# Two of the four weight sums of a seven-product block: from VectorE to a plain load and an adding DMA

## The chip, the cores and the metric

The kernel runs on one core of one Trainium2 chip. A core has TensorE (PE in the profile; PEld is its weight load), VectorE (DVE), ScalarE (ACT), GpSimd (POOL) and SyncE (SP), which here only issues DMAs. The metric is device time in microseconds (us), the median of several runs of the same program.

## What is computed

One inference step of a two-layer transformer backbone on 640 tokens: 512 latent tokens (denoising) and 128 context tokens. Layer 0 mixes with latent-compressed attention and neighbourhood attention, layer 1 with grouped-query attention; each is followed by a gated feed-forward network, and a norm ends it all. The change touches the feed-forward networks:

```python
def swiglu(h, w_in, w_out):
    gate, up = jnp.split(h @ w_in, 2, axis=-1)
    return (jax.nn.silu(gate) * up) @ w_out

xp = xp + g2_p * swiglu(hp, w_ffn_in[l], w_ffn_out[l])
xs = xs + g2_s * swiglu(hs, w_ffn_in[l], w_ffn_out[l])
```

The model width is 1024 and the hidden width 2816, all in fp32.

## The kernel before

Activations stand with features on partitions, tokens on the free axis; the 640 tokens are taken as two halves of 320. fp32 products are made of three matmuls each: weight and activation are split into a rounded high part and the remainder, and high x high, high x low and low x high are added up in PSUM (`mm3`). A weight split is an ACT copy that rounds, and a DVE subtraction (`split`, L1367 and L1368).

**Blocks of seven products.** The first few hidden blocks of a layer are multiplied plainly (4 in layer 0, 3 in layer 1). From there on, a block's product with its 2 x 2 parts (two weight halves for two outputs, two token halves) is made of seven products instead of eight, after Strassen's scheme in the variant of Winograd. This needs sums of weight quarters. A block has a raw tile `ru` (up) and a raw tile `rg` (gate), each 128 x 1024 with two halves of m = 512 columns. `seven` makes four operands of them, each split into high and low: wX = `ru` itself; wW = right half of `rg`; wY = `s13`, two sums; wZ = `s24`, two further sums:

- L1176: s13 left = rg left + rg right
- L1177: s13 right = ru left + rg left
- L1180: s24 left = s13 right + rg right
- L1181: s24 right = s24 left + ru right

All four are DVE additions of 128 x m. `s13` and `s24` are tiles of one tag, `ws`, with two buffers. The matmuls of a block come in the order X, Y, (the W product of the block before, in `close`), Z, X, Z, Y; the profile calls their results `fg`, `fd`, `fu`.

`seven` is called for the blocks of the first feed-forward matrix (the loop from L1481 on: 18 blocks in layer 0, 19 in layer 1), and by `Block` in `ffn_out_seven` for the second matrix of layer 1: three passes (`PASSES`, over 3, 4 and 4 pairs of hidden blocks) with four blocks each, 12 blocks; there m is 384 in the first pass and 512 in the others, and the names in the profile end in o (`ruo`, `rgo`, `s13o`, `wYo`). In all there are 49 blocks.

**Transfers.** Raw weights are loaded by SP: `ru` into one of three buffers `raw`, `rg` into one of these or into a buffer `wr` (two in layer 0, one in layer 1). SP also writes the hidden activations of layer 1 to DRAM (`sp...`, L1398: seven operands a, D, N, b, c, C, E for each pair of blocks) and reads them back for the second matrix (`or...`, `again`, L1278; 320 KB each), a pass's set in turn as buffers come free. POOL issues a few stores of states and none in these stages. Products' operands wY, wZ, wX take turns in six buffers, so the splits run about one block ahead of their use.

**Order.** Each engine's queue is in order. The order in it is not that of the source: a planner sets it when the program is built, by its own times for each instruction and the order of the source as priority; in the trace, for instance, L1176 of block 4 stands on DVE ahead of L1174 of the same block. A load is put where its buffer comes free by the planner's times.

Of the kernel before, what the change touches and what calls it, by code (L numbers as in the profile page):

```python
# [11 lines left out]
F32 = mybir.dt.float32  # L12
F32R = mybir.dt.float32r
AF = mybir.ActivationFunctionType
ALU = mybir.AluOpType
# [3 lines left out]
P = 128  # L19
# [32 lines left out]
def body(ctx, tc, xT, vecs, crow, wm0, wm0g1, wm0g, wm1, wA, wNV, wNA, wMK, wMV, wOA, wGQ, wGK, wGV, wOC,  # L52
         wFI, wFO, wFO1, cckvT, ckrT, cnkT, cnv, cgkT, cgv, rpbp, tabM, tabK, tabG, maskN,
         yT, o_ckvT, o_krT, o_nkT, o_nv, o_gkT, o_gv):
    nc = tc.nc
    V, S, G = nc.vector, nc.scalar, nc.gpsimd
# [32 lines left out]
    def bank(name, kind="m"):  # L89
        if kind == "m":  # L90
            return psp.tile([P, 512], F32, tag="m", bufs=4, name=name)
        return ypool["pool"].tile([P, 512], F32, tag=kind, bufs=ypool["tags"][kind], name=name)
# [13 lines left out]
    def f(ap):  # L106
        return ap.bitcast(F32)
# [55 lines left out]
    def load(src, n, name):  # L163
        raw = rawp.tile([P, 1024], F32, tag="raw", name=name)
        nc.sync.dma_start(raw[:, :n], src)
        return raw[:, :n]
# [177 lines left out]
    def mod0(j, bk, load_):  # L344

        box = []

        def part(half):
            def run():
                if half == 0:  # L350
                    box.append(bk())
                psm, rs = box[0], load_(j, half)

                for g in range(4):
                    for b in range(2):
                        o = 512 * (g % 2) + 256 * b
                        rows = slice(64 * b + 32 * (g % 2), 64 * b + 32 * (g % 2) + 32)
                        PE.matmul(psm[rows, :256], scol[:, 4 * half + g, :], rs[g // 2][:, o:o + 256], start=half == 0 and g < 2,
                                  stop=half == 1 and g > 1, tile_position=(0, rows.start))
                if half == 1:  # L360
                    box.append(tp.tile([P, HT], F32, tag="u", bufs=7, name=f"modsb{j}"))
                    S.activation(box[1][:, :256], psm[:, :256], AF.Copy)
            return run

        def end():
            psm, sb = box
            for i in range(2):
                PE.matmul(psm[:, 4 * i:4 * i + 4], sb[:, i * P:(i + 1) * P], sel, start=True, stop=True)
            for i, t in enumerate(MOD0[j]):
                V.tensor_tensor(mods[0][:, t:t + 2, :], psm[:, 0:8].rearrange("p (a i b) -> p a i b", a=2, b=2)[:, :, i, :],  # L370
                                bc2(bmod(0, t, 2)), ALU.add)
        return [part(0), part(1), end]
# [139 lines left out]
    with tc.tile_pool(name="start", bufs=1) as big:  # L512
# [14 lines left out]
        m = [mod0(j, lambda j=j: bank(f"mod{j}", "m"), lambda j, half: [raws[j, half][:, q, :] for q in range(2)]) for j in range(4)]  # L527
# [91 lines left out]
    for kk in range(4):  # L619
# [3 lines left out]
        for j in range(2):  # L623
            k = 2 * kk + j
            a, b = wh[:, 512 * j:512 * (j + 1)], wl[:, 512 * j:512 * (j + 1)]
            for i in range(5):
                c0, c1 = P * i, P * i + P
# [256 lines left out]
    for h in range(8):  # L884
        p, r = divmod(h, 2)
# [116 lines left out]
    for h in range(8):  # L1002
        p, r = divmod(h, 2)
# [159 lines left out]
                w.append(unit(wFI[l, 0, i], 1024, f"wgu{l}_{i}", "vg"[i], pool=fp))  # L1163
        return ph, fk, dr, hd, fs, fp, w, (su, scratch), pre

    def seven(ru, rg, name, fp, split):

        n = ru.shape[-1]
        m = n // 2
        wX = split(ru, f"wX{name}")  # L1170
        t = fp.tile([P, 2, 512], F32R, tag="w4", bufs=2, name=f"wW{name}")
        wW = t[:, 0, :m], t[:, 1, :m]
        S.activation(wW[0], rg[:, m:], AF.Copy)
        V.tensor_tensor(wW[1], rg[:, m:], f(wW[0]), ALU.subtract)  # L1174
        s13 = fp.tile([P, 1024], F32, tag="ws", bufs=2, name=f"s13{name}")[:, :n]
        V.tensor_tensor(s13[:, :m], rg[:, :m], rg[:, m:], ALU.add)  # L1176
        V.tensor_tensor(s13[:, m:], ru[:, :m], rg[:, :m], ALU.add)  # L1177
        wY = split(s13, f"wY{name}")
        s24 = fp.tile([P, 1024], F32, tag="ws", bufs=2, name=f"s24{name}")[:, :n]
        V.tensor_tensor(s24[:, :m], s13[:, m:], rg[:, m:], ALU.add)  # L1180
        V.tensor_tensor(s24[:, m:], s24[:, :m], ru[:, m:], ALU.add)  # L1181
        wZ = split(s24, f"wZ{name}")
        return wX, wW, wY, wZ

    def ffn_out_seven(x, nxt, opened, ops, spilt, split, close, last):
# [6 lines left out]
        def raw(n, c0, m, name):  # L1192
            raws[0] += 1
            t = (rawp.tile([P, 1024], F32, tag="raw", name=name) if raws[0] % 4 else
                 fp.tile([P, 1024], F32, tag="wr", bufs=1, name=name))[:, :m]
            nc.sync.dma_start(t, wFO1[n, :, c0:c0 + m])
            return t
# [9 lines left out]
        def result(n, c, src, sign, end):  # L1207

            o = HALF[c][0]
            for c0, c1, i in HCOND[c]:  # L1210
                V.scalar_tensor_tensor(x[n][:, c0:c1], src[:, c0 - o:c1 - o],
                                       ng[:, n, i:i + 1] if sign < 0 else mods[1][:, G2 + n, i:i + 1], x[n][:, c0:c1], ALU.mult, ALU.add)
            if end:
                nrm.add(x[n], c)

        class Block:


            def __init__(self, i, n, c0):
                self.pairs, self.n, self.name = PASSES[i], n, f"o{i}_{n}"  # L1220
                self.end = i == len(PASSES) - 1
                self.m = m = P * len(self.pairs)
                ru, rg = raw(n, c0, 2 * m, f"ru{self.name}"), raw(n + 4, c0, 2 * m, f"rg{self.name}")
                self.wX, self.wW, self.wY, self.wZ = seven(ru, rg, self.name, fp, split)
                self.held = {}

            def go(self, ps, wt, j, what, first):
# [20 lines left out]
                    self.copy("p5", self.b5)  # L1248

            def p6(self):  # L1250
                self.go(self.g, self.wZ, 0, "N", False)
                self.copy("u2", self.g)

            def p2(self):
# [2 lines left out]
                result(self.n, 0, self.add("p1", b2), 1, self.end)  # L1257

            def p3(self):
                self.go(self.b5, self.wZ, 1, "c", False)  # L1260
                result(self.n, 1, self.add("u2", self.b5), 1, self.end)

            def p7(self, ready=True):
# [27 lines left out]
        prev, c0 = None, 0  # L1291
# [28 lines left out]
        e0, e1 = ends  # L1320
# [12 lines left out]
        for b in ends:  # L1333
# [4 lines left out]
                nrm.rstd(0)  # L1338
            t = weighed[b.n + 4] = tp.tile([P, HT], F32, tag="u", bufs=7, name=f"xw{b.n}")
            S.activation(t, x[b.n + 4][:, HT:T], AF.Copy, scale=vcol(V_NFIN + b.n + 4))  # L1340
        e0.go(e0.b5, e0.wZ, 1, "c", False)
        result(e0.n, 1, e0.b5, 1, True)
        e1.go(e1.b5, e1.wZ, 1, "c", False)
        sq = tp.tile([P, HT], F32, tag="u", bufs=7, name="fn1sqe")
        parts = []
        for c0, c1, i in HCOND[1]:
# [10 lines left out]
    def ffn(l, x, pend, hm, nxt, side, opened):  # L1357
# [3 lines left out]
        def split(src, name):  # L1361

            turn[0] += 1
            t = (wp, fp)[turn[0] % 2].tile([P, 2, 1024], F32R, tag="w", bufs=3, name=name)
            n = src.shape[-1]
            h, w_ = t[:, 0, :n], t[:, 1, :n]
            S.activation(h, src, AF.Copy)  # L1367
            V.tensor_tensor(w_, src, f(h), ALU.subtract)  # L1368
            return h, w_
# [5 lines left out]
        def product(ps, wt, w0, which, first):  # L1375
            for k, (h, l_) in enumerate(hm.operand(which)):
                a, b = [w[:, w0 + k * P:w0 + k * P + P] for w in wt]
                mm3(ps[:, :HT], a, b, h, l_, first and k == 0, k == 3, skip_group_check=not first)
# [102 lines left out]
        for fb in range(few, FB):  # L1481

            ru = load(wFI[l, fb, 1], 1024, f"wu{l}_{fb}r")
            if fb == few or l and fb % 2:
                rg = load(wFI[l, fb, 0], 1024, f"wg{l}_{fb}r")
            else:
                rg = fp.tile([P, 1024], F32, tag="wr", bufs=2 - l, name=f"wg{l}_{fb}r")
                nc.sync.dma_start(rg, wFI[l, fb, 0])
            wX, wW, wY, wZ = seven(ru, rg, f"{l}_{fb}", fp, split)

            g, b5, b2 = bank(f"fg{l}_{fb}"), bank(f"fd{l}_{fb}"), bank(f"fu{l}_{fb}", "y")
            up, sg = tmp(f"up{l}_{fb}"), tmp(f"sg{l}_{fb}")
            p1, p5, u1, g2 = [utile(f"{n}{l}_{fb}") for n in ("p1", "p5", "u1", "g2")]
            product(g, wX, 0, 11, True)
            S.activation(p1, g[:, :HT], AF.Copy)
            product(b5, wY, 0, "D", True)
            S.activation(p5, b5[:, :HT], AF.Copy)  # L1497
            if job:
                close(job)
            product(g, wZ, 0, "N", False)  # L1500
            S.activation(u1, g[:, :HT], AF.Copy)
            product(b2, wX, 512, 21, True)
            V.tensor_tensor(up[:, 0:HT], b2[:, :HT], p1, ALU.add)
            product(b5, wZ, 512, 22, False)
            V.tensor_tensor(up[:, HT:T], b5[:, :HT], u1, ALU.add)
            product(g, wY, 512, "C", False)
            V.tensor_tensor(g2, g[:, :HT], p5, ALU.add)
            S.activation(sg[:, HT:T], g2, AF.Silu, scale=-1.0)
            job = fb, g, wW, up, sg
# [48 lines left out]
        pss, ws = {}, {}  # L1558
# [127 lines left out]
    ws = [unit(wGK[v], 1024, f"wgk{v}") for v in range(2)]  # L1686
# [198 lines left out]
    _, before = mod_side([(1, wm1[G2:], G2)], None)  # L1885
# [172 lines left out]
```

## Time and profile before

| | |
|---|---|
| median of 3 runs | 1502.37 us (1499.85 to 1502.47) |
| the profiled execution | 1503.23 us, its span 1501.2 us |
| DMA | 231.48 MB, mean 154 GB/s |
| HBM | 193.15 MB read, 36.66 MB written |
| SP's queue | 225.43 MB, 45.0% of 16 engines' span |
| POOL's queue | 0.93 MB, 0.2% |
| granted TensorE clock | 0.995 |

The profile is of one execution. The span runs from the first to the last instruction; times of rows are counted from its start. Rows of the timeline give start, length, engine, source line, operation, `output<-inputs`, shapes and a count where like instructions are merged. DMA rows give the size and the microseconds from issue to landing. The layer-0 blocks run from about 451 to 643 us, those of layer 1 from 1120 to 1354 us, the output blocks from 1351 to 1490 us.

### The profile page before, as it was taken

To read this page: it belongs to the slowest core of one execution; us is meant where nothing else is said; L and a number is where in the kernel's file an instruction comes from. 1 tells how busy PE (TensorE), PEld (TensorE's weight loads), DVE (VectorE), ACT (ScalarE), POOL (GpSimd) and SP (SyncE) were. 2 spreads that over 40 slices of the span, in tenths; PEclk is the share of its full clock that TensorE was granted. 3 is DMA by queue.
4 is the path that set the end of the run, shared out by engine and by line. 5 is a ranking of instruction groups with operands and counts; after the bars stand their busy time and mean duration, and the time that the engine had idled before them with its cause. 6 is when DMAs were issued, how large, how long until landed. Compare 5 with 4: busy or idle time off the path is not lost. (4 is left out here: it accounts for less than half of the span.)

```text
span 1501.2 us, 25833 instructions
## 1 busy us (share of the span) xinstructions
PE 1448.7 (96%) x9766; PEld 1392.8 (93%) x9766; DVE 1233.7 (82%) x2375; ACT 786.2 (52%) x1539; POOL 176.3 (12%) x272
## 2 busy tenths in 40 slices
PE   5999989899999999999999999999999999999997
PEld 4989978889899999999999999989899999999996
DVE  5877778877788888955898887887899989889976
ACT  5446677763635555532122656673565555655443
POOL 0046636420000000000000122220100000000000
PEclk9999999999999999999999999999999999999999
DMA  9653341015055555549775311115245555548561
GB/s 375 202 152 121 114 145 43 15 64 204 29 207 164 170 171 168 162 169 341 231 229 169 103 33 36 37 41 185 68 157 169 193 170 191 175 154 297 181 263 71
DMA packets 79636, 231.48 MB, mean 154 GB/s; under 512 B 8856, under 2 KB 13240, under 8 KB 79128
## 3 DMA queue, kind: packets, MB, share of 16 engines
q1 hardware_dynamic: 77152, 225.43, 45.0%
q10 hardware_dynamic: 1944, 3.48, 0.7%
q8 instruction: 76, 1.25, 0.3%
q0 software_dynamic: 416, 0.93, 0.2%
q14 instruction: 48, 0.39, 0.1%
HBM read 193.15 MB, written 36.66 MB: 153 GB/s over the span
## 5 line engine op out<-in xcount | busy, mean ns | idle before, releaser
L1627 DVE SCALAR_TENSOR_TENSOR junk<-wm,cb 128x1024 bf16<-128x1024 f32 x88 | 107.2, 1218 | 3.4 <-DMA wm<-in_wm 2.8
L64 PE MATMUL gq<-h10h,wgq 128*128 128x320 f32 x256 | 65.8, 316 | 0.0
L261 POOL TENSOR_SCALAR h10h<-h10t,gs,mods 128x320 fp32r<-128x320 f32 x4 | 3.1, 787 | 437.7 <-DVE h10t L255 435.4
L1367 ACT ACTIVATE wY<-s 128x1024 fp32r<-128x1024 f32 x37 | 39.2, 1060 | 27.7 <-PE fg L64 24.0
L1893 POOL TENSOR_TENSOR xr<-xw,fn1rs 128x320 f32<-128x320 f32 x2 | 1.7, 860 | 416.9 <-ACT fn1rs L229 416.9
L1367 ACT ACTIVATE wZ<-s 128x1024 fp32r<-128x1024 f32 x37 | 39.1, 1057 | 18.6 <-PE fd L64 16.3
L1368 DVE TENSOR_TENSOR wZ<-s,wZ 128x1024 fp32r<-128x1024 f32 x37 | 45.2, 1222 | 2.9 <-ACT wZ L1367 0.2
L1476 DVE TENSOR_TENSOR sg<-up,sg 128x640 f32<-128x640 f32 x37 | 30.4, 822 | 20.8 <-ACT sg L1475 20.3
L64 PEld LDWEIGHTS gq<-h10h,wgq 128*128 128x128 f32 x256 | 44.9, 189 | 0.6
L1368 DVE TENSOR_TENSOR wY<-s,wY 128x1024 fp32r<-128x1024 f32 x37 | 45.1, 1218 | 0.3
L1475 ACT ACTIVATE sg<-fg 128x320 f32<-128x320 f32 x37 | 16.2, 438 | 48.5 <-PE fg L64 48.5
L64 PE MATMUL fg<-h01q,wgu 128*128 128x320 f32 x192 | 40.3, 316 | 0.9 <-ACT h01q L298 0.5
L1497 ACT ACTIVATE p<-fd 128x320 f32<-128x320 f32 x37 | 16.2, 438 | 46.7 <-PE fd L64 46.7
L1830 ACT ACTIVATE gp<-gs,gb,rq 128x640 f32<-128x640 f32 (+1 forms) x40 | 31.8, 795 | 15.3 <-DVE gb L1829 13.6
L64 PE MATMUL gq<-h10l,wgq 128*128 128x320 f32 x128 | 39.5, 308 | 0.0
L64 PE MATMUL fg<-h11q,wX 128*128 128x320 f32 x228 | 36.7, 309 | 0.0
L64 PE MATMUL fu<-h11q,wX 128*128 128x320 f32 x228 | 36.6, 309 | 0.0
L64 PE MATMUL fd<-h11q,wZ 128*128 128x320 f32 x228 | 36.6, 309 | 0.0
L64 PE MATMUL fg<-h11E,wW 128*128 128x320 f32 x228 | 36.5, 309 | 0.0
L64 PE MATMUL fg<-h11N,wZ 128*128 128x320 f32 x228 | 36.5, 309 | 0.0
L64 PE MATMUL fd<-h11D,wY 128*128 128x320 f32 x228 | 36.4, 308 | 0.0
L64 PE MATMUL fg<-h11C,wY 128*128 128x320 f32 x228 | 36.4, 308 | 0.0
(3399 smaller groups left out, 5323.0 us busy)
## 6 DMA issues: line engine op xcount, KB each, us to landing
wm<-in_wm SPq DMA_DIRECT2D x48, 512.0 KB, 4.2
mraw<-in_wm SPq DMA_DIRECT2D x8, 1024.0 KB, 13.1
mraw<-in_wm SPq DMA_DIRECT2D x16, 512.0 KB, 4.1
wmv<-in_wm0g SPq DMA_DIRECT2D x8, 512.0 KB, 3.9
wm<-in_wm0g SPq DMA_DIRECT2D x8, 512.0 KB, 5.3
ruo<-in_wFO SPq DMA_DIRECT2D x8, 512.0 KB, 4.0
rgo<-in_wFO SPq DMA_DIRECT2D x8, 512.0 KB, 6.0
x<-in_xT SPq DMA_DIRECT2D x8, 320.0 KB, 5.2
```

What stands on the lines that cost most here:

```text
L64: cls.last = nc.tensor.matmul(*a, **k)
L261: G.tensor_scalar(h[:, c0:c1], t, self.gsl[:, k, 0:1], self.ml[:, self.sh + k, 0:1], ALU.mult, ALU.add)
L1367: S.activation(h, src, AF.Copy)
L1368: V.tensor_tensor(w_, src, f(h), ALU.subtract)
L1475: last = S.activation(sg[:, 0:HT], g[:, :HT], AF.Silu, scale=-1.0)
L1476: V.tensor_tensor(sg, up, sg, ALU.mult)
L1497: S.activation(p5, b5[:, :HT], AF.Copy)
L1627: V.scalar_tensor_tensor(junk, raw, 1.0, cb[:, c, :], ALU.mult, ALU.mult, accum_out=mods[l][:, j0 + i, c:c + 1])
L1830: S.activation(dst, src, AF.Exp, bias=nb, scale=rq[:, j:j + 1], accum_out=ll[:, j:j + 1])
L1893: G.tensor_tensor(x[k][:, c0:c1], root[1][k], nrm.rs[:, c0:c1], ALU.mult)
```

## The change

`first_sums` makes s13 without DVE: SP loads the right half of the gate weights into the left half of the tile and the left half of the up weights into its right half; then POOL issues one DMA that adds the left half of the gate weights, read twice (a source step of 0), onto both halves. Of the gate weights only the right half (`gb`) is loaded as a tile of its own. The two other sums are made on DVE in place in the same tile, after wY has been split from it, so `s24` is gone and a block uses one `ws` buffer instead of two; its halves stand the other way round, so the products that take wZ swap their column offsets.

```diff
+    def first_sums(name, fp, m, gb, ua, ga):
+
+        t = fp.tile([P, 1024], F32, tag="ws", bufs=2, name=f"s13{name}")[:, :2 * m]
+        nc.sync.dma_start(t[:, :m], gb)
+        nc.sync.dma_start(t[:, m:], ua)
+        G.dma_start(t.rearrange("p (i c) -> p i c", i=2), bass.AP(tensor=ga.tensor, offset=ga.offset, ap=[ga.ap[0], [0, 2], ga.ap[1]]),
+                    accum_op=ALU.add)
+        return t
+
-    def seven(ru, rg, name, fp, split):
+    def seven(ru, gb, s13, name, fp, split):
...
-        S.activation(wW[0], rg[:, m:], AF.Copy)
-        V.tensor_tensor(wW[1], rg[:, m:], f(wW[0]), ALU.subtract)
-        s13 = fp.tile([P, 1024], F32, tag="ws", bufs=2, name=f"s13{name}")[:, :n]
-        V.tensor_tensor(s13[:, :m], rg[:, :m], rg[:, m:], ALU.add)
-        V.tensor_tensor(s13[:, m:], ru[:, :m], rg[:, :m], ALU.add)
+        S.activation(wW[0], gb, AF.Copy)
+        V.tensor_tensor(wW[1], gb, f(wW[0]), ALU.subtract)
         wY = split(s13, f"wY{name}")
-        s24 = fp.tile([P, 1024], F32, tag="ws", bufs=2, name=f"s24{name}")[:, :n]
-        V.tensor_tensor(s24[:, :m], s13[:, m:], rg[:, m:], ALU.add)
-        V.tensor_tensor(s24[:, m:], s24[:, :m], ru[:, m:], ALU.add)
-        wZ = split(s24, f"wZ{name}")
+        V.tensor_tensor(s13[:, m:], s13[:, m:], gb, ALU.add)
+        V.tensor_tensor(s13[:, :m], s13[:, m:], ru[:, m:], ALU.add)
+        wZ = split(s13, f"wZ{name}")
...
-                ru, rg = raw(n, c0, 2 * m, f"ru{self.name}"), raw(n + 4, c0, 2 * m, f"rg{self.name}")
-                self.wX, self.wW, self.wY, self.wZ = seven(ru, rg, self.name, fp, split)
+                ru, gb = raw(n, c0, 2 * m, f"ru{self.name}"), raw(n + 4, c0 + m, m, f"rg{self.name}")
+                s13 = first_sums(self.name, fp, m, wFO1[n + 4, :, c0 + m:c0 + 2 * m], wFO1[n, :, c0:c0 + m], wFO1[n + 4, :, c0:c0 + m])
+                self.wX, self.wW, self.wY, self.wZ = seven(ru, gb, s13, self.name, fp, split)
...
-                rg = load(wFI[l, fb, 0], 1024, f"wg{l}_{fb}r")
+                gb = load(wFI[l, fb, 0, :, 512:], 512, f"wg{l}_{fb}r")
             else:
-                rg = fp.tile([P, 1024], F32, tag="wr", bufs=2 - l, name=f"wg{l}_{fb}r")
-                nc.sync.dma_start(rg, wFI[l, fb, 0])
-            wX, wW, wY, wZ = seven(ru, rg, f"{l}_{fb}", fp, split)
+                gb = fp.tile([P, 1024], F32, tag="wr", bufs=2 - l, name=f"wg{l}_{fb}r")[:, :512]
+                nc.sync.dma_start(gb, wFI[l, fb, 0, :, 512:])
+            s13 = first_sums(f"{l}_{fb}", fp, 512, wFI[l, fb, 0, :, 512:], wFI[l, fb, 1, :, :512], wFI[l, fb, 0, :, :512])
+            wX, wW, wY, wZ = seven(ru, gb, s13, f"{l}_{fb}", fp, split)
...
-            product(g, wZ, 0, "N", False)
+            product(g, wZ, 512, "N", False)
...
-            product(b5, wZ, 512, 22, False)
+            product(b5, wZ, 0, 22, False)
```

In `ffn_out_seven` the offsets of wZ change in the same way (p6 takes 1, p3 and the two last products take 0).

More of the change, by code (lines that the diff above doesn't have):

```diff
@@ L1250, in p6 @@
             def p6(self):
-                self.go(self.g, self.wZ, 0, "N", False)
+                self.go(self.g, self.wZ, 1, "N", False)
                 self.copy("u2", self.g)
@@ L1259, in p3 @@
             def p3(self):
-                self.go(self.b5, self.wZ, 1, "c", False)
+                self.go(self.b5, self.wZ, 0, "c", False)
                 result(self.n, 1, self.add("u2", self.b5), 1, self.end)
@@ L1340, in ffn_out_seven @@
             S.activation(t, x[b.n + 4][:, HT:T], AF.Copy, scale=vcol(V_NFIN + b.n + 4))
-        e0.go(e0.b5, e0.wZ, 1, "c", False)
+        e0.go(e0.b5, e0.wZ, 0, "c", False)
         result(e0.n, 1, e0.b5, 1, True)
-        e1.go(e1.b5, e1.wZ, 1, "c", False)
+        e1.go(e1.b5, e1.wZ, 0, "c", False)
         sq = tp.tile([P, HT], F32, tag="u", bufs=7, name="fn1sqe")
```

## The prediction

> **What bounds the kernel now.** I read the busy shares of the page first, then the windows of the stages that the change touches, then the waits of TensorE (PE), then the DMA queues.
>
> ```profile
> span 1501.2 us, 25833 instructions
> PE 1448.7 (96%) x9766; PEld 1392.8 (93%) x9766; DVE 1233.7 (82%) x2375; ACT 786.2 (52%) x1539; POOL 176.3 (12%) x272
> ```
>
> ```profile
> 452.00:640.00 188.00, 188.00 (x1285) 188.00 (x1284) 166.81 (x239) 98.55 (x154) 0.00 (x0) 1.00 0.52 166
> 1130.00:1340.00 210.00, 210.00 (x1435) 210.00 (x1433) 190.06 (x304) 123.62 (x216) 0.00 (x0) 1.00 0.51 168
> 1340.00:1400.00 60.00, 60.00 (x412) 59.98 (x411) 54.74 (x100) 30.88 (x53) 0.00 (x0) 1.00 0.86 297
> 1428.00:1452.00 24.00, 24.00 (x166) 24.00 (x165) 15.57 (x28) 8.65 (x13) 0.00 (x0) 1.00 1.02 387
> 1452.00:1484.00 32.00, 31.72 (x215) 31.19 (x213) 25.08 (x48) 13.99 (x26) 0.00 (x0) 1.00 0.01 4
> ```
>
> The columns are the stretch, its length, busy time of PE, weight load, VectorE (DVE), ScalarE (ACT), GpSimd (POOL), granted clock, DMA share, GB/s. In the two long seven-product stretches (452 to 640 and 1130 to 1340) PE is busy in every microsecond. DVE is busy for 89% and 91% of them, but a DVE second is worth nothing where PE never waits. In the list of PE's waits, those that DVE ends in and around these stages are short (in all, times, longest):
>
> ```profile
> PE fn1pe L64 <- DVE fn1acc L208: 0.9, 1, 0.9
> PE fu_3a L64 <- DVE wgu L174: 0.9, 1, 0.9
> PE fg L64 <- DVE g L1507: 0.9, 1, 0.9
> ```
>
> The second is at the start of layer 0's blocks; the others end a stage, behind a chain that the sums aren't in.
>
> The second thing to see is the DMA share. It is half in the long stretches, 0.86 in 1340 to 1400, and 1.02 in 1428 to 1452, where the last pass of the output product reads its operands back; right after it, it is 0.01.
>
> **What the change removes.** In each of 49 blocks (18, 19 and 12) it takes the two sums of L1176 and L1177 from DVE.
>
> ```profile
> L1176 DVE TENSOR_TENSOR s13o<-rgo 128x512 f32<-128x512 f32 (+1 forms) x12 | 7.7, 638 | 0.0
> ...
> L1177 DVE TENSOR_TENSOR s13o<-ruo,rgo 128x512 f32<-128x512 f32 (+1 forms) x12 | 7.6, 637 | 0.0
> ```
>
> That is 15.3 us for the 12 output blocks, and in the 37 others 2 x 0.68 us (the row at 434.05 below), so 50 us: some 66 us of DVE in all. On the path of PE only one piece of it lies, the 0.9 us of fu_3a. DVE ahead of it:
>
> ```profile
> 434.05 0.68 DVE L1176 TENSOR_TENSOR s<-wg_4r 128x512 f32<-128x512 f32 x1
> ...
> 438.06 1.22 DVE L174 TENSOR_TENSOR wgu<-wgu_31r,wgu 128x1024 fp32r<-128x1024 f32 x1
> ```
>
> ```profile
> 435.74 1.05 ACT L173 ACTIVATE wgu<-wgu_31r 128x1024 fp32r<-128x1024 f32 x1
> ```
>
> ACT has the high part ready at 436.79, DVE takes it up 1.27 us later because sums stand in its queue. Two sums of up to 0.68 us gone ahead of it make up for that, and the 0.9 us of PE go: **-0.9 us**. What is late next is ACT's high part, and that was in time for PE by the same 1.27 us.
>
> **What it adds.** Per block of 512 columns: two SP loads of 256 KB, one adding DMA of 512 KB issued by POOL, and 256 KB less of the gate weights; net 768 KB more. The split of wY now waits for both transfers in turn, and the two other sums wait for that split, since they overwrite its source; behind them come wZ's split and the release of the raw tile. Does PE notice? Block 13 of layer 1:
>
> ```profile
> 1228.30 1.93 PE L64 MATMUL fg<-h11q,wX 128*128 128x320 f32 x12
> ...
> 1240.61 1.92 PE L64 MATMUL fg<-h11q,wX 128*128 128x320 f32 x12
> ```
>
> ```profile
> 1241.40 1.21 DVE L1368 TENSOR_TENSOR wZ<-s,wZ 128x1024 fp32r<-128x1024 f32 x1
> 1242.53 1.21 DVE L1368 TENSOR_TENSOR wY<-s,wY 128x1024 fp32r<-128x1024 f32 x1
> ```
>
> A block takes 12.31 us, so block 14 starts at 1252.92; its wY (ready at 1243.74) is used one product (1.76 us) later, its wZ three products later, at 1258.2. In the new order: wY ready 1243.7, two sums 1.4, wZ's two splits 2.3, so wZ at 1247.4, still 10.8 us early. The sum tile has two buffers, so block 16's plain load starts at 1247.4. The split of its wY can begin when that buffer comes free, with the last product of block 14, which ends two blocks after 1240.61, at 1265.2, so the two transfers have nearly 18 us before anything moves and about 11 more before PE does. What they take has only these rows near it:
>
> ```profile
> out_o_nv<-nvf POOLq DMA_DIRECT2D x1, 256.0 KB, 6.3
> ...
> wg_14r<-in_wFI SPq DMA_DIRECT2D x2, 512.0 KB, 5.1
> ```
>
> The plain load is worth the second row, 5.1 us. No row shows an adding DMA. Below, it can't beat the plain 5.1 us; above, I bound it by twice POOL's 6.3 us, 12.6, since it must fetch the tile as well as the source. The row nearest is the POOL one, so I take 6 to 7 us: 12 of these us are used, and even the upper bound (17.7) just fits. So the 37 blocks cost **0**, and their cover is this lead. The queues behind: on SP, the waiting load stands ahead of the spills and of the next raw load; on POOL nothing else stands in these stretches (0.00 busy), and its issue is short.
>
> **Where the traffic shows.** In 1428 to 1452 the queues are full and PE follows the reloads closely:
>
> ```profile
> 1440.75 0.32 SPq L1278 DMA_DIRECT2D or7c<-sp7c  x1
> ...
> 1444.07 0.32 SPq L1278 DMA_DIRECT2D or7C<-sp7C  x1
> 1444.89 0.33 SPq L1196 DMA_DIRECT2D rgo<-in_wFO  x1
> ```
>
> ```profile
> or7c<-sp7c SPq DMA_DIRECT2D x1, 320.0 KB, 6.6
> ...
> or7C<-sp7C SPq DMA_DIRECT2D x1, 320.0 KB, 6.5
> ```
>
> ```profile
> 1447.71 0.61 PE L64 MATMUL fdo<-or7c,wZo 128*128 128x320 f32 x3
> ...
> 1451.51 0.60 PE L64 MATMUL fgo<-or7C,wYo 128*128 128x320 f32 x3
> ```
>
> or7c lands at 1447.35 and is used 0.36 us later; or7C lands at 1450.57 and is used 0.94 us later. A reload of 320 KB is issued each 0.82 us (1444.07 to 1444.89), so 256 KB are worth 0.66 us. Which of the new transfers fall in here? The sum tile of the last pass's third block is free when wZ of its first is split; wY of that one, now:
>
> ```profile
> 1426.91 1.21 DVE L1368 TENSOR_TENSOR wYo<-s13o,wYo 128x1024 fp32r<-128x1024 f32 x1
> ```
>
> wY is done at 1428.1, the sums at about 1430, wZ at about 1432.7. Its plain load (two of 256 KB) then enters SP ahead of the reloads c and C: 1.3 us. Its adding DMA follows some 6.6 us later, at about 1440, before the last reloads: 1.3 us if it costs what a plain 512 KB costs, 2.6 if the fetch of the tile counts like a second transfer; I take 2.6, by what it has to move. The adding DMA of the second block's sums starts at about 1424 and overlaps the beginning of the burst: 0 to 1.3, I take half, 0.65. Together 4.55 us later for the last reload; less its slack of 0.94, PE stands **+3.6 us**. Bounds: 0 (all of it behind the reloads, as rgo stands at 1444.89) to 1.3 + 2.6 + 1.3 - 0.36 = 4.8. After 1452 PE is busy to the tail, so nothing gives this back.
>
> [...]
>
> **The sum.** -0.9 + 3.6 = +2.7 us on the profiled execution, 1503.23 us (its span is 1501.2, with 2.0 around it): 1505.9. The median of the runs shown is 1502.37, 0.86 lower; beside it the forecast is 1505.1.
>
> **Rivals.**
> (a) The traffic is hidden: the planner puts the third block's loads behind the reloads, or they arrive in a gap. For it: rgo, which the reloads outrank, stands behind them all. Against it: the new loads need no raw tile and are free about 6 us before the last reloads. Then -0.9 stays, 1501.5, and at most the three waits of the list go, 2.7 us: 1499.7. An order of the queues that happens to come out better still is what I leave for faster.
> (b) Slower, by one mechanism: the two transfers in series come too late for the second pass of the output product, where the share is already 0.86. Its first block has the least lead:
>
> ```profile
> 1363.56 0.95 DVE L1368 TENSOR_TENSOR wZo<-s24o,wZo 128x768 fp32r<-128x768 f32 x1
> ...
> 1385.13 1.22 DVE L1368 TENSOR_TENSOR wYo<-s13o,wYo 128x1024 fp32r<-128x1024 f32 x1
> ```
>
> ```profile
> 1390.57 0.59 PE L64 MATMUL fdo<-or0D,wYo 128*128 128x320 f32 x3
> ```
>
> The tile is free about 1369.5 (wZ of two blocks before now follows its wY and the sums). A full-queue landing of 6.6 us gives 1376.1. The adding DMA and wY's split (2.3) must end by 1390.57, so it decides from an adding DMA of 12 us on, and each further microsecond costs PE one: at 14 to 20 us, +2 to +8 on top of the forecast, 1507 to 1513. Far beyond that the long stretches would go as well: past 18 + 11 us of transfers the loop over two blocks sets the period. For it: no row shows an adding DMA, and the queues are full there. Against it: twice POOL's row is 12.6.
> That the change doesn't take the work off DVE I give no chance: the instructions are gone.
>
> **How the numbers follow.** A measurement of this kernel tells about 0.2% (3.0 us) from no change. Forecast 0.5; its own range, a stall of 0.9 to 4.8 us (with less it is (a)) and -0.9 on the median, is 1502.4 to 1506.3, of which 0.27 lies within 0.2% and 0.23 above. (a) 0.22: 0.15 within, 0.07 faster. (b) 0.28: 0.03 within, 0.25 slower. So faster 0.07, same 0.45, slower 0.48. The range leaves out half of what is faster and half of (b), its upper part: 1499.7 to 1511.0.
>
> **What would show it.** Right: no PE idle in 452 to 640 and 1130 to 1340; DVE's busy time down by about 66 us; the wait of fu_3a on wgu gone; a new wait of PE on a DMA of or4c to or7C near 1447 to 1452, of 2 to 4 us; DMA bytes up by about 37 MB. Wrong: a wait of ACT on the sum tile inside the long stretches followed by idle PE, an adding DMA of over 12 us to landing, or a late wY at 1390.

## The result and the profile after

| | before | after |
|---|---|---|
| median | 1501.84 us (1499.85 to 1502.47, 4 runs) | 1522.86 us (1520.95 to 1524.52, 4 runs) |
| ratio, 95% interval | | 1.0142 [1.0123, 1.0160] |
| profiled execution, its span | 1503.23, 1501.2 us | 1520.95, 1519.2 us |

The change costs 21 us where 2.7 were forecast, and the time lies outside the range. First the busy line and the DMA queues on the page of after:

```profile
span 1519.2 us, 26241 instructions
...
PE 1453.6 (96%) x9766; PEld 1395.8 (92%) x9766; DVE 1181.1 (78%) x2277; ACT 778.2 (51%) x1539; POOL 236.6 (16%) x321
...
q1 hardware_dynamic: 91264, 238.02, 46.5%
q0 software_dynamic: 13744, 26.10, 10.3%
```

DVE is busy 52.6 us less, and 37.8 MB more are moved. The q0 row is POOL's queue: packets, MB, share of 16 engines' span. Now the windows of after, with the columns explained in the prediction:

```profile
452.00:640.00 188.00, 188.00 (x1285) 188.00 (x1284) 146.14 (x206) 92.78 (x148) 18.13 (x15) 1.00 0.83 227
1130.00:1340.00 210.00, 210.00 (x1435) 210.00 (x1434) 171.19 (x269) 121.28 (x217) 21.72 (x18) 1.00 0.83 233
1340.00:1380.00 40.00, 40.00 (x274) 39.94 (x274) 32.05 (x61) 19.77 (x37) 2.41 (x2) 1.00 0.96 315
1380.00:1420.00 40.00, 29.89 (x171) 29.05 (x170) 21.31 (x35) 12.47 (x19) 3.63 (x3) 0.83 0.79 236
1440.00:1460.00 20.00, 19.98 (x137) 19.71 (x135) 14.03 (x23) 7.60 (x13) 1.20 (x1) 1.00 1.01 340
1460.00:1480.00 20.00, 19.52 (x128) 18.76 (x129) 11.45 (x23) 6.95 (x12) 2.41 (x2) 1.00 0.93 275
```

and of before, for two of these windows that the prediction doesn't show:

```profile
1380.00:1420.00 40.00, 40.00 (x275) 40.00 (x274) 39.49 (x68) 18.18 (x26) 0.00 (x0) 1.00 0.62 208
1440.00:1460.00 20.00, 20.00 (x138) 20.00 (x137) 13.41 (x26) 8.09 (x15) 0.00 (x0) 1.00 0.63 244
```

Look at the count of matmuls behind the busy time of PE. The two long stretches are untouched. In 1380 to 1420, the second pass of the output product, PE gets through 171 matmuls for 275. At 40 / 275 = 0.145 us each, the missing 104 are 15 us of the 18 by which the span grew. PE's busy time fell by only 10 us there: the other 5 are in the granted clock, 0.83. PE comes to the last reloads late, so they stand in 1460 to 1480 (128 matmuls for 139 before): it is 13.4 us behind before at the row of or7b (1459.37 for 1445.95) and 15.0 behind at that of or7C (1466.50 for 1451.51), so they cost it 1.6 us. (At 1330 it had been 1.9 us ahead, so 13.4 and not 15.) The other 3 of the 18 us are lost behind them, in the last two blocks and the norm. The list of PE's waits in 1335 to 1519 (in all, times, longest) names what it waited for:

```profile
PE fgo L64 <- ACT u2o L1238: 5.9, 1, 5.9
PE fdo L64 <- ACT wYo L1373: 3.6, 1, 3.6
...
PE fdo L64 <- DVE wYo L1374: 0.6, 1, 0.6
PE fgo L64 <- DVE wXo L1374: 0.4, 1, 0.4
PE fdo L64 <- DMA or4c<-sp4c: 0.2, 1, 0.2
```

**The first wait.** Rows of the timeline of after, in order of time:

```profile
1372.80 0.33 SPq L1169 DMA_DIRECT2D s13o<-in_wFO  x1
1373.57 0.33 SPq L1170 DMA_DIRECT2D s13o<-in_wFO  x1
...
1382.48 1.20 POOL L1171 DMA_DIRECT2D s13o<-in_wFO  x1 [21.39 <-DVE wXo L1374]
...
1385.15 0.60 PE L64 MATMUL fdo<-op10c,wZo 128*128 128x320 f32 x3
...
1390.22 1.06 ACT L1373 ACTIVATE wYo<-s13o 128x1024 fp32r<-128x1024 f32 x1 [7.70 <-DMA or0C<-sp0C]
1391.18 0.42 ACT L1238 ACTIVATE u2o<-fgo 128x320 f32<-128x320 f32 x1
...
1391.66 1.17 PE L64 MATMUL fgo<-op9C,wYo 128*128 128x320 f32 x3 [5.91 <-ACT u2o L1238]
...
1392.62 1.00 PE L64 MATMUL fgo<-or8C,wYo 128*128 128x320 f32 x3
```

The loads of the pass's first block enter SP at 1372.8, POOL issues the adding DMA 9.7 us later (the first load alone took 8.2 us to land), and ACT takes up wY another 7.7 us later: 17.4 us from load to sum. PE, however, isn't stopped where it needs wY. On ACT, behind the waiting split, stands u2o, the copy that frees a PSUM bank: the product it copies ended at 1383.12, but it starts at 1391.18, after the split; PE stands still from 1385.75 to 1391.66 for that. (The releaser in the bracket of wYo, or0C, had nothing to do with the tile; it was only the last DMA to land before it.) The three matmuls of a row then take 1.00 us for 0.60, a row each 0.80 us for 0.44, until 1395.64: the granted clock was 0.53 in 1391.66 to 1395.64.

**The second wait** comes from the first:

```profile
1385.84 0.41 SPq L1284 DMA_DIRECT2D or2C<-sp2C  x1
...
1394.49 0.32 SPq L1284 DMA_DIRECT2D or3C<-sp3C  x1
...
1395.39 0.37 SPq L1169 DMA_DIRECT2D s13o<-in_wFO  x1
...
1401.83 1.20 POOL L1171 DMA_DIRECT2D s13o<-in_wFO  x1 [18.14 <-DVE wWo L1183]
...
1411.00 1.06 ACT L1373 ACTIVATE wYo<-s13o 128x1024 fp32r<-128x1024 f32 x1 [9.01 <-DMA s13o<-in_wFO]
```

SP stands for 8.2 us at or3C, which takes the buffer of an operand that the stalled products have yet to read. Behind it stand the next block's loads. Their chain takes 15.6 us, and PE waits 3.6 us for wYo. The landings, the median from issue, in the first matrices (s) and in the output blocks (s13o):

```profile
s<-in_wFI SPq DMA_DIRECT2D x74, 256.0 KB, 3.9
s<-in_wFI POOLq DMA_DIRECT2D x37, 512.0 KB, 7.6
s13o<-in_wFO POOLq DMA_DIRECT2D x8, 512.0 KB, 7.2
```

So an adding DMA is not slower in the output blocks by its median, 7.2 us for 7.6. Of the two chains above, the first lost its time in the plain loads (8.2 us for 3.9) and had an adding DMA of 7.7 us; the second had loads of 4.0 and 5.4 us and an adding DMA of 9.1.

### The profile page after: what moved, and what is told of

It is laid out like the page before. It is cut to its first block, busy times and chain, and to the rows that moved or that the text cites. A ratio compares the mean times of both kernels' runs of the same rounds, so it can differ in the third digit from the quotient of the medians.

```text
span 1519.2 us, 26241 instructions
## 1 busy us (share of the span) xinstructions
PE 1453.6 (96%) x9766; PEld 1395.8 (92%) x9766; DVE 1181.1 (78%) x2277; ACT 778.2 (51%) x1539; POOL 236.6 (16%) x321
## 4 chain that ended last, share of the span: by engine, by line
PE 77%; DVE 8%; DMA 6%; ACT 5%; issue 2%; POOL 1%; ACTq 0%; DVEq 0%; SPq 0%; POOLq 0%
PE fg L64 19%; PE fd L64 8%; PE fo L64 5%; PE fu L64 4%; PE fgo L64 3%; PE gq L64 3%; PE fdo L64 2%; PE nk L64 2%; PE go L64 2%; PE gs L64 2%; PE nq L64 2%; DMA s13o<-in_wFO 1%; DMA mraw<-in_wm 1%; PE ms L64 1%; PE gt L68 1%
## 5 line engine op out<-in xcount | busy, mean ns | idle before, releaser
L1171 POOL DMA_DIRECT2D s<-in_wFI x37 | 44.9, 1213 | 525.9 <-DMA s<-in_wFI 193.3
L1171 POOL DMA_DIRECT2D s13o<-in_wFO x12 | 14.5, 1206 | 148.7 <-DVE wXo L1374 59.1
L64 PE MATMUL fg<-h01C,wY 128*128 128x320 f32 x216 | 34.6, 309 | 1.6 <-ACT u L1508 1.6
L64 PE MATMUL fg<-h01E,wW 128*128 128x320 f32 x216 | 34.7, 309 | 0.0
```

Source lines behind the costliest of these rows:

```text
L64: cls.last = nc.tensor.matmul(*a, **k)
L1171: G.dma_start(t.rearrange("p (i c) -> p i c", i=2), bass.AP(tensor=ga.tensor, offset=ga.offset, ap=[ga.ap[0], [0, 2], ga.ap[1]]), accum_op ...
```

## The experiments

**Theory A**: the chain of two transfers is late for the output product's second pass, and only that. **Rivals**: B, the traffic itself slows the stage; C, the in-place sums; D, the add in the DMA. Two kernels split the change by place:

```diff
# layers only: Block as before (seven_sums is the seven of before); output only: the reverse
-                self.wX, self.wW, self.wY, self.wZ = seven(ru, gb, s13, self.name, fp, split)
+                self.wX, self.wW, self.wY, self.wZ = seven_sums(ru, rg, self.name, fp, split)
```

> The change in the 37 blocks of the first feed-forward matrices alone; the 12 output blocks as before. Theory A (the chain of a plain load and an adding DMA comes too late for the first blocks of the output product's second pass, behind the burst of reloads on SP; the first matrices only gain): 1.9 us under the kernel before, 1499.9 us, since PE stands 1.93 us ahead of before at 1330 us in the trace of the change. Theory B (the added traffic costs wherever it is): 28 of the 38 added MB are here, so about +15 us. Theory C (the in-place sums wait for the split of wY and delay wZ): 37 of 49 blocks, +10 us or more.

Measured: 1502.53 us, ratio 1.0004 [0.9994, 1.0013]. No loss, and no gain that can be measured from 50 us less of DVE: B's 15 us and C's 10 fell, and theory A's 1.9 us of gain didn't come either.

> The change in the 12 output blocks alone; the first matrices as before. Theory A: the whole loss and none of the gain, 1501.8 + 18.0 + 1.9 = about 1522 us, with PE waits of 5 to 6 us behind ACT's copy u2o near 1386 us and of about 4 us for wYo near 1402 us. Theory B: 9.4 of 38 MB, +5 us. Theory C: 12 of 49 blocks, +5 us.

Measured: 1518.87 us, 1.0125 [1.0112, 1.0139], 17.7 us over the 1501.15 of before. PE's waits:

```profile
PE fgo L64 <- ACT u2o L1257: 7.7, 1, 7.7
PE fdo L64 <- ACT wYo L1392: 2.8, 1, 2.8
```

The loss is in the 12 output blocks, with both waits in their places; it is 3 us less than theory A's figure and over three times those of B and C. The next kernels start from this one ("output only") or from before.

```diff
# in place alone: before, all 49 blocks
-        s24 = fp.tile([P, 1024], F32, tag="ws", bufs=2, name=f"s24{name}")[:, :n]
-        V.tensor_tensor(s24[:, :m], s13[:, m:], rg[:, m:], ALU.add)
-        V.tensor_tensor(s24[:, m:], s24[:, :m], ru[:, m:], ALU.add)
+        V.tensor_tensor(s13[:, m:], s13[:, m:], rg[:, m:], ALU.add)
+        V.tensor_tensor(s13[:, :m], s13[:, m:], ru[:, m:], ALU.add)
```

> Loads and all four DVE sums as before in all 49 blocks; only the third and fourth sum are made in place in the tile of the first two. Theory A: within 1.5 us of before (1500.3 to 1503.3), since the waits seen after the change are for transfers and not for the split of wY. Theory C: +10 us or more.

Measured: 1511.71 us, 1.0071 [1.0054, 1.0087]: theory A's figure fell, C's held. The largest of DVE's waits in 1130 to 1340 and of PE's from the first blocks on:

```profile
DVE wZ L1367 <- ACT wZ L1366: 18.1, 16, 1.2
```

```profile
PE fg L64 <- DVE g L1506: 3.4, 6, 0.9
```

With all four sums still on DVE, the queue that this edit gives makes DVE wait at the head for ACT's wZ (before, no such row), 18 us in a stretch where it had 20 to spare, and PE comes to wait for it. In after the same wait stands there (20.1 us, 17 times), but DVE has 39 of the 210 us to spare, and layers only, in place too, loses nothing. So C is a real price in the first matrices, covered in the change by DVE's freed time. In the output blocks it is small: from 1360 to 1460 this kernel gets through 679 matmuls for 684 before, 0.7 us. C is not the cause of the 21 us.

```diff
# no add: output only
-                    accum_op=ALU.add)
+        )
```

> As the change in the output blocks alone, but POOL's DMA writes and does not add, so the two sums it makes are not the reference's: same bytes from HBM, same order and waits. Theory A: the chain of two transfers stays, landing of POOL's transfer 6 to 9 us as with the add, 1515 to 1523 us. Theory D (the add itself is slow): POOL's transfer lands in 4 us or less and the time falls to 1500 to 1506 us.

Measured: 1512.26 us, 1.0079 [1.0064, 1.0094], between the two figures. Queue and landing rows, first with the add (output only), then without:

```profile
q0 software_dynamic: 3680, 6.70, 2.5%
...
s13o<-in_wFO POOLq DMA_DIRECT2D x8, 512.0 KB, 7.8
```

```profile
q0 software_dynamic: 2016, 6.70, 1.3%
...
s13o<-in_wFO POOLq DMA_DIRECT2D x8, 512.0 KB, 5.3
```

The same bytes take half the engine time without the add. 0.93 MB and 0.2% of the queue are other stores, as in before. With the add it is 5.77 MB in 2.3% of 1516.1 us, 165 GB/s; without, 5.77 MB in 1.1% of 1508.9, 348 GB/s. The page of after, with 25.17 MB of adds in 10.1% of 1519.2 us, gives 164; SP's queue before, 225.43 MB in 45.0% of 1501.2, gives 334. By these rates, as an estimate, 512 KB with the add take 3.2 us of the engines' time as the queue row counts it, a plain transfer of that size 1.5 to 1.6. D is a part: 6.6 of 17.7 us, through engine time and the earlier landing (5.3 us for 7.8) together.

```diff
# traffic alone: before, with unread transfers by POOL in blocks 2 to 11, in two halves h
+                        t = tmp(f"by{self.name}{h}")[:, :m]
+                        G.dma_start(t[:, :k], wFO1[n + 4, :, c0 + m + h * k:c0 + m + h * k + k])
+                        G.dma_start(t[:, k:], wFO1[n, :, c0 + h * k:c0 + h * k + k])
+                        ga = wFO1[n + 4, :, c0 + h * k:c0 + h * k + k]
+                        G.dma_start(t.rearrange("p (i c) -> p i c", i=2),
+                                    bass.AP(tensor=ga.tensor, offset=ga.offset, ap=[ga.ap[0], [0, 2], ga.ap[1]]), accum_op=ALU.add)
```

> The kernel before, with nothing of its own changed; beside each of ten output blocks (all but the first two) POOL also makes the two plain loads and the adding DMA of the change, in two halves, into a scratch tile that nobody reads: the added traffic and the adds, without anybody waiting for them. Theory A (what is late is the chain): 1501 to 1504 us, no PE wait of more than 1 us. Theory B (the traffic and the adds slow the other transfers): 1510 us or more, since the change in the output blocks alone takes 1518.9.

Measured: 1512.18 us, 1.0068 [1.0056, 1.0081]. Theory A as it stood fell: 10.2 us go though nobody waits for the new transfers. In this kernel the 512 KB loads of rgo in the output stage land in 10.1 us, against 6.0 before; the row, and two windows:

```profile
rgo<-in_wFO SPq DMA_DIRECT2D x8, 512.0 KB, 10.1
```

```profile
1380.00:1420.00 40.00, 38.20 (x250) 38.05 (x250) 38.13 (x66) 17.14 (x26) 19.03 (x24) 0.96 1.07 323
1440.00:1460.00 20.00, 18.15 (x90) 15.10 (x88) 7.11 (x13) 4.26 (x8) 5.83 (x9) 0.83 1.08 359
```

The DMA share is 1.07 and 1.08, and PE loses 25 matmuls (3.6 us) in the first window and 48 (7.0 us) in the last reloads. PE is idle for only 3.7 us of these 10.6; in the rest its matmuls run slower: at half the rate for some us in both windows (granted clock 0.96 and 0.83), and in the second at the pace of the reloads. In the first window the delay starts with the raw tile ruo, for which ACT waits 4.7 us; in the second PE waits for the reloads. The extra load is somewhat more than the change's: 1024 KB per block, where the change adds 768 net.

Three kernels move the chain in the output blocks (block (1,0) is the first of the second pass): loads on POOL's queue (`G.dma_start` for the two `nc.sync.dma_start` of `first_sums`); one order fixed; and that order with an earlier place on SP:

```diff
# u2 first: block (1,0) alone
-        wY = split(s13, f"wY{name}")
+        wY = after(gate, lambda: split(s13, f"wY{name}"))     # gate: the copy u2o of the block before
# early: as u2 first, and Block(i, 0, c0) is made ahead of a pass's reloads
+                ahead = Block(i, 0, c0)
                 for what in PRODUCTS:
```

> The change in the output blocks alone, with its two plain loads issued by POOL ahead of the adding DMA, so that they no longer stand behind the reloads on SP. Theory A: the chain of block (1,0) starts about 4 us earlier, the one of block (1,1) about 15 us earlier; the PE wait near 1382 us falls from 7.7 to 2 to 4 us, that near 1407 us goes, 1505 to 1510 us. Rival (the two transfers in series are too long wherever they start): 1516 us or more.

Measured: 1518.70 us, 1.0123 [1.0103, 1.0142]: nothing gained. The waits near 1382 are shorter (1.5 and 3.2 us), but others stand in the last reloads, where the granted clock is 0.89. The rival's figure held, but not all the waits are for the two transfers.

> The change in the output blocks alone, with one order fixed: the ACT half of the split wY of block (1,0) stands behind the copy u2o of the block before it, on which PE waited 7.7 us. SP's order is the same. Theory A: PE waits for wYo itself instead, 5 to 6 us; but the reloads or3C and the loads behind it on SP come about 7 us earlier, and the second wait near 1407 us goes: about 1512 us. Rival (ACT's order alone makes the first wait): the first wait goes as well, 1505 us or less. Rival (order is no matter): 1518 us.

Measured: 1517.50 us, 1.0103 [1.0089, 1.0116]. The wait moved as theory A had it (3.1 us for wYo, and none near 1407), but new ones for p1o came later, and the time is that of the third rival, order is no matter:

```profile
PE fgo L64 <- ACT p1o L1259: 3.1, 2, 2.3
PE fdo L64 <- ACT wYo L1396: 3.1, 1, 3.1
```

> As the run before with the fixed order, and the loads of block (1,0) moved ahead of eight reloads in SP's queue, where they then wait only for their buffer. Theory A: the sum of block (1,0) is there in time, no PE wait near 1385 us; the chain of block (1,1) still starts behind or3C, takes about 18 us to wY, and PE leaves it about 15 us: one wait of 3 to 5 us near 1400 us, 1507 to 1511 us. Rival (the add is late wherever it is put): 1512 us or more.

Measured: 1514.16 us, 1.0082 [1.0068, 1.0097]. The first wait is gone, the second is there as expected, 3.9 us for wYo; the time is 3 us above the expected, in the rival's range. It is 12.2 us over its own before (1501.97), so this order gives back 5.5 of 17.7 us; a better one wasn't tried. That asked for **theory E**: the stage has no DMA time left. Before and after, the stage as a whole:

```profile
1340.00:1460.00 120.00, 120.00 (x821) 119.98 (x820) 104.24 (x184) 56.70 (x92) 0.00 (x0) 1.00 0.73 256
```

```profile
1340.00:1460.00 120.00, 109.87 (x714) 108.70 (x713) 83.20 (x144) 48.20 (x78) 9.66 (x8) 0.94 0.87 272
```

Before, it used 0.73 of 120 us, 88 us. Per block of 512 columns the change makes 1024 KB plain (3.1 us of all engines at 334 GB/s) into 1280 KB plain and 512 KB with an add (3.9 + 3.2): 4.0 us more. Eight such blocks and two of 384 columns (3.0) come to 38: by this estimate 126 us for 120. That by itself asks for 6 us of the 17.7. And after's engines aren't full where PE stands: the share is 0.79 in 1380 to 1420, behind 0.96 in 1340 to 1380.

```diff
# half reloads: output only, and (control) before
-            nc.sync.dma_start(f(t), spilt[p, what])
+            nc.sync.dma_start(f(t)[:, 0:HT], spilt[p, what][:, 0:HT])
```

> The change in the output blocks alone, with each reload of an operand cut to its left half, 160 KB for 320, and the products using the left half twice (so the output blocks' result is not the reference's); the same number of matmuls, the chain of two transfers as it was. New theory E (the output stage has no DMA time left: before, the engines were busy 0.73 of 1340 to 1460 us, 88 us of 120; the change adds some 4 us of all 16 engines to each 12 us block, since the adding DMAs move 165 GB/s where plain ones move 335): without 9 MB of reloads, some 27 us, there is room again, 1500 to 1506 us and no wait over 1.5 us. Rival (the two transfers in series are too long for the lead by themselves): 1511 us or more.

> The control: the kernel before with the same halved reloads (the output blocks' result is not the reference's). Both theories: 1499 to 1503 us, since before the reloads were hidden.

Measured: 1507.51 us, 1.0044 [1.0027, 1.0062], and the control 1503.16 us, 1.0011 [1.0000, 1.0023], at the upper end of what was expected. The change in the output blocks costs 4.4 us with half the reloads, 17.7 with all. With the changed form, then the control:

```profile
1380.00:1420.00 40.00, 37.61 (x257) 37.35 (x256) 29.76 (x49) 17.16 (x26) 4.80 (x4) 1.00 0.79 211
1440.00:1460.00 20.00, 17.49 (x114) 17.23 (x113) 11.18 (x19) 7.03 (x12) 2.41 (x2) 0.96 0.84 221
```

```profile
1380.00:1420.00 40.00, 40.00 (x275) 40.00 (x275) 36.93 (x64) 17.80 (x26) 0.00 (x0) 1.00 0.51 153
1440.00:1460.00 20.00, 18.87 (x127) 18.34 (x126) 16.64 (x28) 9.26 (x16) 0.00 (x0) 1.00 0.21 69
```

Theory E's figure was 1500 to 1506 with no wait over 1.5 us; two waits of 2.5 us on p1o, behind a late wY on ACT, are left. The rival's 1511 fell too. Most of the loss goes with the reloads; but with fewer reloads the chain also lands earlier (the loads of s13o in 4.4 us for 5.5, the adding DMA in 6.9 for 7.8), and the planner's order of the loads differs in these two kernels, so this run doesn't part the chain from the traffic.

```diff
# plain traffic: traffic alone, POOL's second transfer without accum_op
# more traffic: layers only, behind each adding DMA, for j in 0, 1
+                after(adds[-1], lambda: G.dma_start(dr.tile([P, 1024], F32, name=f"by{l}_{fb}{j}"), wFI[l, fb, j]))
```

> The kernel before with the unread transfers beside ten output blocks, as in the run that took 1512.2 us, but POOL's second transfer writes and does not add. Theory E: the adds' extra 1.6 us of engine time per block is gone, 1503 to 1508 us. Rival (the bytes from HBM count, not the add): 1511 to 1513 us.

Measured: 1509.11 us, 1.0050 [1.0033, 1.0066], between the two figures; the interval overlaps that of the adding form, so what the add contributes to unread traffic stays open.

> The change in the first matrices alone (1502.5 us), and behind each adding DMA POOL also copies two 512 KB weight tiles from DRAM to DRAM, which nobody reads or waits for. DMA share of those stages is 0.80 to 0.83; the copies add 3.1 us or more of all engines per 12.3 us block. Theory E: the share would pass 1, the blocks become DMA-bound and stretch by 7% or more: 1530 us or more. Rival (only lateness against the lead of about 18 us counts, and nobody waits for the copies): 1502 to 1510 us.

Measured: 1523.58 us, 1.0139 [1.0117, 1.0161], 21 us over layers only, where 28 or more were expected. The profile is of the slowest of four executions, 1534.57 us, so its waits are larger than at the median. Windows, a landing that is 3.9 in after, and the largest of PE's waits:

```profile
452.00:640.00 188.00, 179.74 (x1202) 178.17 (x1201) 137.31 (x191) 88.16 (x141) 33.56 (x45) 0.98 0.94 293
1130.00:1340.00 210.00, 206.11 (x1389) 203.24 (x1387) 159.78 (x248) 108.98 (x198) 36.95 (x48) 1.00 0.94 305
```

```profile
s<-in_wFI SPq DMA_DIRECT2D x74, 256.0 KB, 8.5
```

```profile
PE fg L64 <- DVE g L1537: 14.8, 14, 4.2
```

A second wait, 5.8 us once, is for the copy u on ACT. At a DMA share of 0.83 the first matrices hide the change; at 0.94 they no longer do, though the copies are read by nobody.

## Why the prediction was wrong

- **Removed work, -0.9 us.** The wait of fu_3a is gone. That 66 us of DVE are worth nothing more was right: layers only is at 1.0004. DVE's busy time fell by 52.6 us, not 66: added up row by row its instructions are 61.8 us shorter (1365.7 to 1303.8), and busy time counts the overlap of neighbouring rows only once.
- **The 37 blocks, 0.** Right, and for the reason given. The adding DMA lands in 7.6 us (6 to 7 taken), the loads in 3.9 (5.1 taken): 11.5 of the 18 us of lead. What the step didn't say is how far this cover goes: it held at a DMA share of 0.83 and was gone at 0.94.
- **The second pass of the output product at nothing: the step that failed.** The sum has one term for the new transfers, "Where the traffic shows", +3.6 us, and counts only those that fall into 1428 to 1452, because there the share was 1.02. The 0.86 of 1340 to 1400 was taken to carry the others for nothing, and a late wY there was left to rival (b). Measured, 15 us are lost in 1380 to 1420, by two late wY and the waits behind them. The unread traffic alone costs 3.6 us there. The sum of engine time over the stage, 88 + 38 us for 120, was at hand but for the add, and the prediction's 2.6 us for 512 KB "by what it has to move" was near the 3.2 that the rates of POOL's queue give.
- **The term that was counted, +3.6 us.** In the change the last reloads cost PE 1.6 us, in waits of PE and its weight loads on or4c to or7c, 0.2 to 0.4 us each. The place and the kind of wait were right, the size was less than half; PE comes there 13.4 us late, and the loads behind it too. With the unread traffic, where PE comes earlier, the same place loses 7.0 us, half of it to the clock (granted 0.83).
- **What the counted term took for granted.** No run shows it as it was added up: that POOL's transfers delay SP's, and that an adding DMA of 512 KB is worth 2.6 us to them, were the author's estimates, and no row of before has a transfer of POOL's beside SP's reloads. What the runs showed in its place: in the traffic run POOL's transfers alone took SP's rgo from 6.0 to 10.1 us, and POOL's queue moved 165 GB/s with the add and 348 without.
- **Rival (b), +2 to +8 us on top.** Its place was right, the first block of the second pass, with a due time of 1390.57. Its price was not. It let the loads start at 1369.5 and land in 6.6 us, and so asked for an adding DMA of 12 us. In fact they start at 1372.8, behind reloads on SP, and POOL follows 9.7 us later; 7.7 us of adding DMA were then enough. Nor did it see what stands behind the waiting instruction on ACT (u2o, so that PE stops 5 us before it needs wY), nor what stands behind PE on SP (or3C and the next block's loads), nor the clock. The prediction looked at the queues behind the new waits on SP and on POOL, and left out ACT's.
- **The clock** was in no step. It is 5 of the 15 us in 1380 to 1420, and, by the rows at half the rate (3.8 us and 7.1), some 5 of the 10.6 that the unread traffic takes in its two windows.

What is shown: the loss is in the output blocks (1.0004 and 1.0125), most of it behind two late wY of the second pass; traffic that nobody waits for makes 10.2 us there (medians); the add, in the chain, 6.6 of 17.7; one better order gives back 5.5; with half the reloads 4.4 of 17.7 are left. These overlap and are not terms of a sum. What stays open is how much of the 17.7 is traffic and how much the serial chain as such, since whatever made the transfers land sooner shortened the chain too. A sum tile of its own for the last two sums, with the DMAs kept, wasn't tried. No version beat the kernel before.

## What to carry to other kernels

Before work goes from an engine to the DMAs, add up the DMA engines' time stage by stage (share x length, plus each new transfer at its own rate: here 165 GB/s for an adding one, 334 to 348 for a plain one) and compare it with the stage's length: here 0.73 of 120 us was no room for 38 us more. That is a condition, not the price: 6 us too many, by that estimate, went with a loss of 17.7. Look at every in-order queue that gets a new wait, ACT included, and ask which evacuation stands behind it: here u2o, for 5.9 us of PE. A freed engine that isn't waited for paid for nothing here: 50 us of DVE less in layers only left the time at 1.0004.

## What the runs showed of the hardware

Several waits here cost PE more than its idle time: behind them matmuls ran at about half the rate, a row of three each 0.80 us for 0.44. After the 5.9 us of the first wait they did so from 1391.66 to 1395.64 (granted clock 0.53), after the second, of 3.6 us, from 1413.80 to 1419.36 (0.51). In the traffic run a wait of 1.8 us was followed by 3.8 us of it:

```profile
1381.82 1.02 PE L64 MATMUL fgo<-op9E,wWo 128*128 128x320 f32 x3 [1.79 <-DVE p5o L1245]
1382.64 1.00 PE L64 MATMUL fgo<-or8E,wWo 128*128 128x320 f32 x3
...
1385.66 0.60 PE L64 MATMUL fgo<-op10N,wZo 128*128 128x320 f32 x3
```

With half the reloads a wait of 2.4 us near 1384 was followed by a granted clock of 1.00, but one of 2.5 us near 1458 by 3.8 us of slow matmuls; so the length of the wait alone doesn't tell. The slow matmuls lasted 3.8 to 4.0 us after three of these waits and 5.6 after the fourth. In the first wait the clock fell while PE still stood: from 1388.80 to 1395.60 the granted clock was 0.51, and PE was busy for 3.9 of these 6.8 us. What sets the fall and the return was not shown.
